# An eighth full set of seven block products, with fewer partner halves spread evenly between them, in a GLA and differential attention layer

## The chip, the cores and the metric

The kernel runs on one core of a Trainium2 chip. The metric is the device time of one launch in microseconds (us). The text names the engines as the profile does: PE is TensorE (PEld its weight loads), DVE is VectorE, ACT is ScalarE, POOL is GpSimd and SP is SyncE. POOL and SP mostly issue DMAs here.

## The reference

One decoder layer on a sequence of 256 tokens and a width of 2048, all in float32. What matters here is how much of it is matrix products:

```
h = rmsnorm(x, pre_norm_g)                       # 256 x 2048
proj = h @ w_in                                  # 2048 columns and more for each of:
(a_q, a_k, a_v, a_g, a_lr, b_q, b_k, b_v, b_g, m_a, m_b) = split(proj)
gk  = log_sigmoid(a_lr @ gla_gk_w2 + gla_gk_b) / 16
o_a = rmsnorm(gla_chunked(a_q, a_k, a_v, gk)) * gla_norm_g * silu(a_g)   # 4 heads
y_a = o_a @ w_branch_a
o_b = rmsnorm(diff_attention(b_q, b_k, b_v, lam)) * diff_norm_g * (1 - 0.2) * silu(b_g)  # 16 heads
y_b = o_b @ w_branch_b
merged = sigmoid(m_a) * y_a + sigmoid(m_b) * y_b
out = x + rmsnorm(merged @ w_out) * post_norm_g
```

The columns a_g, the GLA gates, are called ag0 to ag3 in the kernel (512 columns each). The merge columns m_a are m00 to m03. The queries and keys of the differential heads are dq and dk, in four groups of four heads.

## The kernel before, in words

**Halves.** Weights are read once from DRAM as float32. A float32 product is done as three passes of a reduced-precision one: ScalarE copies a weight tile to the rounded part `hi` (L357), VectorE subtracts it from the tile and keeps the rest `lo` (L358), and TensorE sums hi times the rounded x, hi times the rest of x, and lo times the rounded x. The unit is a *half*, 128 x 1024 weights: one ACT copy, one DVE subtraction, and then the matmuls of L552. All halves stand in one list, `seq` (L208 to L211). `take` (L366) hands out the next half to the matmuls and keeps the splits three halves ahead (`AHEAD`, with three buffers each for hi and lo). `emit_half` (L325) makes the split of one half, and also starts the loads that its place in the list calls for.

**Sets.** Most products h @ w_in are token-major: a half then costs 12 matmuls of 128x512. A *set* computes two groups of 512 columns in a cheaper way: it cuts x and the weights into 2 x 2 blocks and forms seven block products in place of eight (`block_products`, L827, in the order `PRODUCTS` = 1, 3, 5, 6, 2, 7, 4). A half of a set costs 6 matmuls of 128x512 (four with hi, two with lo), and each product of a full set has four halves: two block rows t = 0 and 1, and two halves of each. This text names such a place by product and t, "5.1" for product 5, t = 1. Seven products of 24 matmuls are 168, where two token-major groups take 192. Before, there are seven full sets, 0 to 6, and one *quarter set* that does a quarter of the work of one ag and one merge group (`QUARTER`, ag3 and m02), with two halves for each product.

**The price of a set.** The products need sums of weight blocks. A set has chain tiles in SBUF: a holds block 0 and b block 3, both loaded on POOL's queue by `link` (L224), for the next set's first product during products 7, 4 and 1. After the halves of product 1 are split, `accumulate` (L251, also on POOL's queue) adds block 1 from DRAM onto a, in four pieces of 512 KB for the two tiles (t = 0 and 1), by a DMA that adds into SBUF. Products 1 uses a as loaded, product 5 uses a with block 1 added; products 3 and 7 use b. After product 5's and product 2's halves, and again after 6 and 7, VectorE adds b or the tile c (block 2, loaded by SP's queue into `raws`) onto a (L260), and block 1 is accumulated onto b as well. So product 5's split has to wait for the landing of the accumulates that were issued at product 1.

**Partners.** Between the halves of the sets the list has other halves of w_in, called *partners* here (`others`, L782): the last group of GLA values (v4), the GLA keys and queries, and the differential heads' queries and keys of the groups named in `EARLY`. Their raw tiles come by SP's queue. Except for v4 they are channel-major: their x side is the moving operand, and a half costs 8 matmuls 512 wide and 8 of 256. `phase_steps` (L100) sets the order: after each slot (s, product, t) one partner, but for a list `skip`; in the first four slots one more. Before, there are 105 slots and 88 partners; in sets 1 to 6 a full set of 14 slots has 11 partners (none after 4.0, 2.0 and 1.0; sets 5 and 6 have one less after 4.1), and the quarter set's seven slots have six.

**Evictions and gates.** Products 1, 6, 7 and 4 add into one PSUM bank x. Product 1 and product 5 are copied out to SBUF by ScalarE (`kept`, L871), and VectorE adds those copies to later banks (L874, L878, L882, L886). Sets of merge columns (`MERGE`, sets 0, 1 and 6) end in a Tanh (L837, L845). The others end in a Tanh on ScalarE and one VectorE operation that makes t times (1 + tanh) of it (L840 and L841, and `gate` at L596). The missing factors 1/2 and rstd are put in later, where the heads are normalised. Results are written to DRAM (`spill`, L175 to L179, on POOL's queue) and fetched back when needed. The quarter set's results are fetched as parts and added to the rest of ag3 and m02.

**After the sets** come ag0 to ag3 and m02 as token-major groups, the differential heads of group 3, m03, and then the two branches and the output product. The GLA scores and the attention of the heads are woven into this stretch.

Of the kernel before, what the change touches and what calls it, by code (L numbers as in the profile page):

```python
# [6 lines left out]
F32 = mybir.dt.float32  # L7
# [4 lines left out]
ALU = mybir.AluOpType  # L12
# [17 lines left out]
SETS = 7  # L30
# [3 lines left out]
EARLY = (0, 1, 2)  # L34
# [15 lines left out]
def chunk_plan():  # L50
# [15 lines left out]
    plan.append(("set6", "set", "w_in", [(o + 8192, 1024)]))  # L66
    plan.append((f"set{SETS}", "quarter", "w_in", [(5632, 512), (o + 9216, 512)]))
    for g in range(4):
        plan.append((f"ag{g}", "rest" if g == 3 else "tok", "w_in", [(4096 + 512 * g, 512)]))
# [30 lines left out]
def phase_steps():  # L100
# [7 lines left out]
    skip = [(SETS, 4, 0), (SETS - 1, 4, 1), (SETS - 2, 4, 1)] + [(s, prod, 0) for prod in (4, 2, 1) for s in range(SETS - 1, 0, -1)]  # L108
    skip = skip[: len(slots) + len(front) - len(other)]
    mixed = []  # L110
    for slot in slots:
        mixed += [("set", *slot, h) for h in range(2)]
        for _ in range((slot not in skip) + (slot in front)):
            mixed.append(other.pop(0))
# [29 lines left out]
def hybrid_kernel(ctx: ExitStack, tc, xt, xn, preg, postg, w, w2, gkb, glag, lamv, diffg, ident_d, causal_d, lmask_d, out):  # L144
# [64 lines left out]
    seq += halves_of(*(f"ag{g}" for g in range(4)))  # L209
    seq += halves_of("m02") + heads_order(3) + halves_of("m03", *(f"y0{g}" for g in range(4)))[:-4]  # L210
# [237 lines left out]
    const.tile([P, 24], F32, name="margin")  # L448
# [12 lines left out]
    def norm():  # L461
# [12 lines left out]
        dve.tensor_scalar(out=half_rstd, in0=rstd, scalar1=0.5, scalar2=None, op0=ALU.mult)  # L474
        dve.tensor_scalar(out=minus_half, in0=rstd, scalar1=-0.5, scalar2=None, op0=ALU.mult)
# [120 lines left out]
    def gate(bank, b, dst):  # L596
        t = t2([P, 512], "tanh")
        act.activation(t, bank, AF.Tanh, scale=half_rstd[:, b : b + 1])
        dve.scalar_tensor_tensor(out=dst, in0=t, scalar=1.0, in1=bank, op0=ALU.add, op1=ALU.mult)
# [227 lines left out]
    def block_products(s):  # L827
        x = ps("mm")
        bank = {1: x, 6: x, 7: x, 4: x}
        kept, halves = {}, {}  # L830

        def right_done(b):
# [5 lines left out]
            else:  # L838
                t = t2([P, 512], "tanh")
                act.activation(t, dst, AF.Tanh, scale=half_rstd[:, b : b + 1])  # L840
                dve.scalar_tensor_tensor(out=dst, in0=t, scalar=-1.0, in1=dst, op0=ALU.add, op1=ALU.mult)  # L841

        def left_done(b, src):
            if s in MERGE:
                act.activation(halves["l"][:, b, :], src, AF.Tanh, scale=half_rstd[:, b : b + 1])  # L845
            elif s < SETS:
                act.activation(halves["l"][:, b, :], src, AF.Copy, scale=rstd[:, b : b + 1])
            elif b:
                act.activation(halves["l"][:, b, :], src, AF.Copy)

        for prod in PRODUCTS:
# [4 lines left out]
            for t in range(few):  # L856
                for h in range(2):
                    hi, lo = take(("set", s, prod, t, h))
                    for w, parts in ((hi, (0, 1)), (lo, (0,))):
                        for j in range(2):  # L860
                            kt = 4 * t + 2 * h + j
                            a = operand(prod, kt)
                            for part in parts:
                                first = prod not in (6, 7, 4) and kt == 0 and w is hi and part == 0
# [805 lines left out]
```

## Time and profile before

| | |
|---|---|
| median of 3 runs | 1089.87 us (1087.65 to 1090.18) |
| the profiled execution: its span | 1087.3 us (no other time is given for it) |
| busy, PE / DVE / ACT / POOL | 1079.5 / 930.8 / 720.0 / 154.5 us |
| DMA | 288.21 MB, 265 GB/s in the mean |
| granted TensorE clock | full speed in each of the 40 slices |

The span is the time from the first to the last instruction of one profiled execution. The median of the other runs is 2.6 us above it. A group's row in the profile gives the line, engine, operation, the output and input tiles, how many there were, the busy time and the mean length of one (ns), and behind the second bar the idle time of the engine before them with what ended it. A row of a timeline gives start, length, engine, line, operation and tiles, and in brackets how long the engine was idle before it and what released it. "DMA to landing" gives the time from the issue of a DMA to its last byte.

### The profile page before, as it was taken

Reading aid. Unit: us, or ns where it says so; the run is one execution under the profiler, and the core shown is the slowest. Engines: PE = TensorE matmul, PEld = TensorE weight load, DVE = VectorE, ACT = ScalarE, POOL = GpSimd, SP = SyncE. Lnnn points to the kernel's source line nnn. Section 1 sums busy time; section 2 is a strip of 40 time slices with the busy share of each in tenths; the row PEclk is TensorE's granted clock in tenths of the full one; section 3 lists DMA queues with packets and bytes.
Section 4 is the critical chain, followed back from the end, with each engine's and each line's share of the span. In section 5 each row is a group of like instructions: output and inputs, shape, how many; then the busy total and the mean of one; then the engine's idle time right before and its main releaser. Section 6 shows DMA issues by size and latency. Waiting matters only on the chain.

```text
span 1087.3 us, 15367 instructions
## 1 busy us (share of the span) xinstructions
PE 1079.5 (99%) x5440; PEld 925.4 (85%) x5440; DVE 930.8 (86%) x1295; ACT 720.0 (66%) x1047; POOL 154.5 (14%) x229
## 2 busy tenths in 40 slices
PE   9999999999999999999999999999999999999997
PEld 8999888888888888888888888888888888888886
DVE  7787987979979899798998899877778878889886
ACT  7886766676766767667676465556777767566662
POOL 0201112121121211212102100021011011100000
PEclk9999999999999999999999999999999999999999
DMA  9889869799797997979968656599898898988752
GB/s 351 286 296 331 241 252 295 210 354 224 258 272 213 364 243 269 295 190 365 241 242 248 239 181 208 180 326 324 259 297 258 280 298 261 333 293 264 272 187 104
DMA packets 64941, 288.21 MB, mean 265 GB/s; under 512 B 8480, under 2 KB 11552, under 8 KB 46944
## 3 DMA queue, kind: packets, MB, share of 16 engines
q1 hardware_dynamic: 39520, 183.72, 48.2%
q0 software_dynamic: 24768, 102.77, 34.6%
q8 instruction: 43, 0.70, 0.3%
q10 hardware_dynamic: 576, 0.73, 0.2%
q14 instruction: 34, 0.28, 0.1%
HBM read 260.98 MB, written 26.21 MB: 264 GB/s over the span
## 4 chain that ended last, share of the span: by engine, by line
PE 88%; issue 5%; DMA 4%; DVE 2%; POOL 1%; ACT 0%; POOLq 0%; ACTq 0%; DVEq 0%
PE mm L552 54%; PE bg L552 24%; DMA a<-in_w_dram 2%; PE mm L540 2%; PE bg L540 2%; PE mm L525 1%; PE bg L977 1%; DVE lo L358 1%; DMA b<-in_w_dram 1%; PE bg L525 1%; DMA dl<-dk 1%; PE bg L1145 0%; PE bg L1119 0%; PE bg L444 0%; PE bg L1120 0%
## 5 line engine op out<-in xcount | busy, mean ns | idle before, releaser
L357 ACT ACTIVATE hi<-raw 128x1024 fp32r<-128x1024 f32 (+3 forms) x253 | 259.2, 1031 | 185.8 <-PE bg L552 89.9
L358 DVE TENSOR_TENSOR lo<-raw,hi 128x1024 fp32r<-128x1024 f32 (+3 forms) x255 | 300.3, 1183 | 63.9 <-ACT hi L357 59.3
L552 PE MATMUL mm<-hi,xs 128*128 128x512 f32 (+1 forms) x808 | 204.3, 386 | 0.0
L552 PEld LDWEIGHTS mm<-hi,xs 128*128 128x128 f32 x808 | 149.7, 188 | 25.0 <-ACT hi L357 0.2
L358 DVE TENSOR_TENSOR lo<-a,hi 128x1024 fp32r<-128x1024 f32 x120 | 144.7, 1220 | 23.7 <-ACT hi L357 22.9
L552 PE MATMUL bg<-xs,hi 128*128 128x512 f32 x640 | 164.9, 389 | 0.0
L357 ACT ACTIVATE hi<-a 128x1024 fp32r<-128x1024 f32 x120 | 127.0, 1060 | 47.2 <-PE mm L552 27.4
L552 PEld LDWEIGHTS bg<-xs,hi 128*128 128x128 f32 x640 | 120.3, 188 | 23.4
L552 PE MATMUL mm<-lo,xs 128*128 128x512 f32 (+1 forms) x404 | 113.1, 384 | 0.3 <-DVE lo L358 0.2
L552 PEld LDWEIGHTS bg<-xs,lo 128*128 128x128 f32 x640 | 87.2, 190 | 6.3
L552 PE MATMUL bg<-xs,lo 128*128 128x256 f32 x640 | 89.2, 282 | 0.0
L552 PEld LDWEIGHTS mm<-lo,xs 128*128 128x128 f32 x404 | 75.5, 188 | 14.6 <-DVE lo L358 1.1
L358 DVE TENSOR_TENSOR lo<-b,hi 128x1024 fp32r<-128x1024 f32 x60 | 72.4, 1221 | 6.5 <-ACT hi L357 5.0
L357 ACT ACTIVATE hi<-b 128x1024 fp32r<-128x1024 f32 x60 | 63.5, 1061 | 17.0 <-PE mm L552 14.7
L552 PE MATMUL mm<-hi,oah 128*128 128x512 f32 x128 | 50.8, 397 | 0.0
L552 PE MATMUL mm<-hi,oal 128*128 128x512 f32 x128 | 50.0, 391 | 0.0
L251 POOL DMA_DIRECT2D b<-in_w_dram x30 | 26.0, 869 | 138.5 <-DVE a L260 112.1
L1131 ACT ACTIVATE prob<-prob,mx,score_scale 128x128 f32<-128x128 f32 x64 | 34.3, 539 | 8.2 <-DVE mx L1126 8.0
L552 PE MATMUL mm<-hi,obh 128*128 128x512 f32 x96 | 37.7, 393 | 0.0
L552 PE MATMUL mm<-hi,obl 128*128 128x512 f32 x96 | 37.4, 390 | 0.0
L260 DVE TENSOR_TENSOR a<-a,b 128x1024 f32<-128x1024 f32 x30 | 36.3, 1221 | 0.3
L357 ACT ACTIVATE hi<-c 128x1024 fp32r<-128x1024 f32 x30 | 31.7, 1057 | 7.1 <-PE mm L552 4.9
(417 smaller groups left out, 2066.8 us busy)
## 6 DMA issues: line engine op xcount, KB each, us to landing
raw<-in_w_dram SPq DMA_DIRECT2D x110, 1024.0 KB, 6.8
a<-in_w_dram POOLq DMA_DIRECT2D x30, 512.0 KB, 12.6
c<-in_w_dram SPq DMA_DIRECT2D x30, 512.0 KB, 8.5
b<-in_w_dram POOLq DMA_DIRECT2D x30, 512.0 KB, 8.2
a<-in_w_dram POOLq DMA_DIRECT2D x13, 1024.0 KB, 8.5
b<-in_w_dram POOLq DMA_DIRECT2D x13, 1024.0 KB, 8.6
raw<-in_w_dram SPq DMA_DIRECT2D x14, 832.0 KB, 7.1
gr<-gr POOLq DMA_DIRECT2D x8, 512.0 KB, 7.9
```

The source lines that it names most:

```text
L251: pool.dma_start(chain[s, name, i][:, c], block(s, 1, i)[:, c], accum_op=ALU.add)
L260: dve.tensor_tensor(out=a, in0=a, in1=chain[s, "b", i][:, c] if second else raws[s, i, h], op=ALU.add)
L357: act.activation(hi_t[:, a:b], r[:, a:b], AF.Copy)
L358: dve.tensor_tensor(out=lo_t[:, a:b], in0=r[:, a:b], in1=f32(hi_t[:, a:b]), op=ALU.subtract)
L525: i = pe.matmul(out, lhs, rhs, start=first and n == 0, stop=last and n == len(pairs) - 1, **kw)
L540: i = pe.matmul(banks[g][b][:, :n], a[part][:, P * b : P * b + P], w[:, n * g : n * g + n], start=first, stop=last)
L552: i = pe.matmul(*args, **kw)
L977: pe.matmul(o, xk[:, P * c : P * c + P], xq.rearrange("p (b c t) -> p b c t", b=2, c=4)[:, :, c, :], start=i == 0, stop=i == 1)
L1131: act.activation(prob[m][:, lo:up], prob[m][:, lo:up], AF.Exp, scale=score_scale[:, b : b + 1], bias=mx[:, i : i + 1], accum_out=z[:, i : ...
```

## The change

1. `SETS` becomes 8. Set 7 does ag0 and ag1 (`GLA_GATES`), which leave the token-major part; the quarter set becomes set 8. The results of set 7 are spilled, with the gate already applied, and fetched back where ag0 and ag1 were computed.
2. Partners stand by a fixed table: in a full set after 3.0, 5.1, 6.0, 6.1, 2.1, 7.0, 7.1 and 4.1, which are 8 for a set, and in the quarter set after products 5, 6, 2 and 7, which are 4. `EARLY` is (0, 1), so the heads of group 2 are no longer partners; they follow m02, ahead of those of group 3. There are now 119 slots and 72 partners.
3. Gates are one Silu on ScalarE with rstd as its scale, in place of a Tanh and a VectorE operation. With that the factor 1/2 and rstd are no longer put in at the heads' normalisation, and two small VectorE multiplications go.
4. In sets 1 and later ScalarE's copy of product 1 goes to a second PSUM bank in place of SBUF, and product 2's matmuls add onto it, so VectorE's addition (L882) goes.

The built program has 3628 matmuls of 128x512 where there were 3652; all other matmuls keep their numbers. It has eight loads of ScalarE's function table where there were two (at L385 and L837). In the new ones Silu alternates with the exponential of the attention (L959 of the changed file); between the Tanh of set 6 and the Silu of set 7 none stands. Line numbers shift by four to nine: the subtraction is L362, the copy L361, the accumulate L255.

```diff
-SETS = 7
+SETS = 8
+GLA_GATES = 7
 QUARTER = ("ag3", "m02")
 MERGE = (0, 1, 6)
-EARLY = (0, 1, 2)
+EARLY = (0, 1)
+PARTNERED = ((3, 0), (5, 1), (6, 0), (6, 1), (2, 1), (7, 0), (7, 1), (4, 1))
+LAST_PARTNERED = (5, 6, 2, 7)
...
     plan.append(("set6", "set", "w_in", [(o + 8192, 1024)]))
+    plan.append((f"set{GLA_GATES}", "set", "w_in", [(4096, 1024)]))
     plan.append((f"set{SETS}", "quarter", "w_in", [(5632, 512), (o + 9216, 512)]))
...
-    skip = [(SETS, 4, 0), (SETS - 1, 4, 1), (SETS - 2, 4, 1)] + [(s, prod, 0) for prod in (4, 2, 1) for s in range(SETS - 1, 0, -1)]
-    skip = skip[: len(slots) + len(front) - len(other)]
     for slot in slots:
         mixed += [("set", *slot, h) for h in range(2)]
-        for _ in range((slot not in skip) + (slot in front)):
+        s, prod, t = slot
+        with_partner = prod in LAST_PARTNERED if s == SETS else (prod, t) in PARTNERED
+        for _ in range(with_partner + (slot in front)):
             mixed.append(other.pop(0))
...
-    seq += halves_of(*(f"ag{g}" for g in range(4)))
-    seq += halves_of("m02") + heads_order(3) + halves_of("m03", *(f"y0{g}" for g in range(4)))[:-4]
+    seq += halves_of("ag2", "ag3", "m02") + heads_order(2) + heads_order(3) + halves_of("m03", *(f"y0{g}" for g in range(4)))[:-4]
...
     def gate(bank, b, dst):
-        t = t2([P, 512], "tanh")
-        act.activation(t, bank, AF.Tanh, scale=half_rstd[:, b : b + 1])
-        dve.scalar_tensor_tensor(out=dst, in0=t, scalar=1.0, in1=bank, op0=ALU.add, op1=ALU.mult)
+        act.activation(dst, bank, AF.Silu, scale=rstd[:, b : b + 1])
...
     def block_products(s):
+        seeded = s > 0
...
-                t = t2([P, 512], "tanh")
-                act.activation(t, dst, AF.Tanh, scale=half_rstd[:, b : b + 1])
-                dve.scalar_tensor_tensor(out=dst, in0=t, scalar=-1.0, in1=dst, op0=ALU.add, op1=ALU.mult)
+                act.activation(dst, dst, AF.Silu, scale=minus_rstd[:, b : b + 1])
...
+            elif s == GLA_GATES:
+                gate(src, b, halves["l"][:, b, :])
             elif s < SETS:
...
-                                first = prod not in (6, 7, 4) and kt == 0 and w is hi and part == 0
+                                first = prod not in ((6, 7, 2, 4) if seeded else (6, 7, 4)) and kt == 0 and w is hi and part == 0
...
-                        if prod in (1, 5):
+                        if prod == 1 and seeded:
+                            bank[2] = ps("mm")
+                            act.activation(bank[2], x, AF.Copy)
+                        elif prod in (1, 5):
...
-                            dve.tensor_tensor(out=halves["l"][:, 0, :], in0=out, in1=kept[1], op=ALU.add)
-                            left_done(0, halves["l"][:, 0, :])
+                            if not seeded:
+                                dve.tensor_tensor(out=halves["l"][:, 0, :], in0=out, in1=kept[1], op=ALU.add)
+                            left_done(0, out if seeded else halves["l"][:, 0, :])
...
-            dve.tensor_tensor(out=ssq, in0=ssq, in1=half_rstd, op=ALU.mult)
...
-            dve.tensor_tensor(out=e, in0=e, in1=half_rstd, op=ALU.mult)
...
-    for g in range(4):
+    for g in range(2):
+        gates.append(fetch(gspill[2 * GLA_GATES + g], "ua", u2))
+    for g in (2, 3):
...
-    diff_heads(3)
+    for g in (2, 3):
+        diff_heads(g)
```

VectorE's order in set 5, from the last split of product 1 (the first row, tile a) to the first split of product 5 (the last row, tile a again). In between, b is a split of product 3, raw that of a partner, and the rows with dk or dq belong to the heads. Before:

```order
L358 TENSOR_TENSOR lo_4085<-a_3958,hi_4084 128x1024
L774 TENSOR_TENSOR dk_3986<-dk_3986,rstd_bc 128x256
L358 TENSOR_TENSOR lo_4096<-raw_4082,hi_4095 128x1024
L358 TENSOR_TENSOR lo_4106<-b_3988,hi_4105 128x1024
L358 TENSOR_TENSOR lo_4116<-b_3988,hi_4115 128x1024
L358 TENSOR_TENSOR lo_4129<-raw_4082,hi_4128 128x1024
L358 TENSOR_TENSOR lo_4150<-b_4030,hi_4149 128x1024
L358 TENSOR_TENSOR lo_4162<-b_4030,hi_4161 128x1024
L358 TENSOR_TENSOR lo_4172<-raw_4159,hi_4171 128x1024
L772 TENSOR_TENSOR dk_3986<-bg_4127,dk_3986 128x256
L358 TENSOR_TENSOR lo_4202<-a_3905,hi_4201 128x1024
```

The same stretch of set 5 on VectorE after the change:

```order
L362 TENSOR_TENSOR lo_3622<-a_3494,hi_3621 128x1024
L362 TENSOR_TENSOR lo_3633<-b_3521,hi_3632 128x1024
L783 TENSOR_TENSOR dq_3426<-dq_3426,dh_3613 128x512
L362 TENSOR_TENSOR lo_3645<-b_3521,hi_3644 128x1024
L362 TENSOR_TENSOR lo_3655<-raw_3642,hi_3654 128x1024
L362 TENSOR_TENSOR lo_3668<-b_3563,hi_3667 128x1024
L362 TENSOR_TENSOR lo_3678<-b_3563,hi_3677 128x1024
L362 TENSOR_TENSOR lo_3690<-a_3448,hi_3689 128x1024
```

Between the last split of product 1 and the first of product 5 there were three partners and there is one; a fourth one stood, and stands no more, between 5.0 and 5.1 (behind the last row).

POOL's order in set 6, from the accumulates onto a (L251) to those onto b; gl, dh and dl are spills of results to DRAM. Before:

```order
L251 DMA a_4520<-in_w_dram 128x1024 x2
L251 DMA a_4563<-in_w_dram 128x1024
L178 DMA gl_4669<-gl_4494 128x1024
L251 DMA a_4563<-in_w_dram 128x1024
L251 DMA b_4591<-in_w_dram 128x1024 x2
L251 DMA b_4633<-in_w_dram 128x1024 x2
```

The same on POOL after the change:

```order
L255 DMA a_3979<-in_w_dram 128x1024 x2
L183 DMA gl_4119<-gl_3955 128x1024
L255 DMA a_4025<-in_w_dram 128x1024
L183 DMA dh_4147<-dh_4144 128x512
L183 DMA dl_4149<-dq_3957 128x512
L255 DMA a_4025<-in_w_dram 128x1024
L255 DMA b_4052<-in_w_dram 128x1024 x2
L255 DMA b_4094<-in_w_dram 128x1024 x2
```

The spill of the last set's left half has moved ahead of the third accumulate, and the two spills of a head pair now stand between the third and the fourth.

## The prediction on record

> **What bounds the kernel now.** I read the page's busy times and slices first, then the list of what PE waited for, then windows of the sets, and last the timelines of PE, ACT and POOL around the accumulates. The page of before:
>
> ```profile
> span 1087.3 us, 15367 instructions
> PE 1079.5 (99%) x5440; PEld 925.4 (85%) x5440; DVE 930.8 (86%) x1295; ACT 720.0 (66%) x1047; POOL 154.5 (14%) x229
> PEclk9999999999999999999999999999999999999999
> ```
>
> PE is busy 99% of the span at the full granted clock in all 40 slices. What PE waited for, in us, times, and the longest:
>
> ```profile
> PE bg L444 <- DVE ones_b L441: 1.6, 1, 1.6
> PE bg L1608 <- ACT diag L1607: 1.0, 1, 1.0
> PE mm L552 <- DVE lo L358: 0.4, 2, 0.2
> ```
>
> The first is the start, the second the end; between them PE loses 0.4 us. So the time is the sum of the matmuls, and a change moves it in two ways only: by the number of matmuls, and by new waits of PE. All other engines matter only as far as they make PE wait. How far they are from that, in one 60 us window inside the sets and two short ones in set 5 (columns: length, busy time of PE, PEld, DVE, ACT, POOL, granted clock, DMA share, GB/s):
>
> ```profile
> 480.00:540.00 60.00, 60.00 (x300) 50.98 (x299) 54.47 (x56) 42.42 (x48) 13.67 (x20) 1.00 0.87 273
> 438.00:446.00 8.00, 8.00 (x41) 6.77 (x40) 5.93 (x7) 5.81 (x8) 4.02 (x5) 1.00 1.00 388
> 446.00:462.00 16.00, 16.00 (x84) 13.67 (x82) 12.37 (x14) 10.18 (x13) 1.14 (x2) 1.00 0.93 249
> ```
>
> DVE is 91% busy, ACT 71%, and the DMA engines 87%. Where only plain loads run they move 388 GB/s at a share of 1.00; where the accumulates run (446 to 462) a share of 0.93 moves only 249. The sets live close to what the DMA engines can move.
>
> **What a half and a partner cost.** PE's timeline in set 5, from product 1 to product 3 with one partner (bg) between:
>
> ```profile
> 440.00 1.09 PE L552 MATMUL mm<-hi,xs 128*128 128x512 f32 x4
> 440.93 0.62 PE L552 MATMUL mm<-lo,xs 128*128 128x512 f32 x2
> ...
> 442.74 1.07 PE L552 MATMUL mm<-hi,xs 128*128 128x512 f32 x4
> ...
> 444.10 1.07 PE L552 MATMUL mm<-hi,xs 128*128 128x512 f32 x4
> ...
> 445.46 1.98 PE L552 MATMUL bg<-xs,hi 128*128 128x512 f32 x8
> ...
> 448.23 0.40 PE L552 MATMUL mm<-hi,s4h 128*128 128x512 f32 x1
> ```
>
> A set's half takes 444.10 - 442.74 = 1.36 us for six matmuls, 0.227 us each. A partner takes 448.23 - 445.46 = 2.77 us. The lo matmuls begin 0.93 us after the hi ones.
>
> **Term 1, the matmuls.** The eighth set takes 24 matmuls of 128x512 away: 24 x 0.227 = -5.4 us. All others stay, only in another order.
>
> **Term 2, the accumulates of the full sets.** Partners do two things: they use PE time, and they give the accumulates onto tile a time to land. From the last half of 1.1 to that of 5.1 there were four partners (after 1.1, 3.0, 3.1, 5.0); now there is one (after 3.0). So three go, 3 x 2.77 = 8.3 us. In the rows below POOL issues the last accumulate of sets 1, 2, 4 and 6 and of both halves of the quarter set:
>
> ```profile
> 169.06 0.84 POOL L251 DMA_DIRECT2D a<-in_w_dram  x1 [0.62 <-DVE lo L358]
> 237.31 0.86 POOL L251 DMA_DIRECT2D a<-in_w_dram  x1 [1.01 <-DVE lo L358]
> 374.93 0.85 POOL L251 DMA_DIRECT2D a<-in_w_dram  x1 [1.02 <-DVE lo L358]
> 511.29 1.71 POOL L251 DMA_DIRECT2D a<-in_w_dram  x1
> 572.07 0.90 POOL L251 DMA_DIRECT2D a<-in_w_dram  x1 [5.30 <-DVE lo L358]
> 573.20 0.88 POOL L251 DMA_DIRECT2D a<-in_w_dram  x1 [0.24 <-DVE lo L358]
> ```
>
> PE uses that piece in the last half of product 5 of the same set:
>
> ```profile
> 190.93 0.39 PE L552 MATMUL mm<-hi,r1h 128*128 128x512 f32 x1
> 259.73 0.39 PE L552 MATMUL mm<-hi,r1h 128*128 128x512 f32 x1
> 397.35 0.39 PE L552 MATMUL mm<-hi,r1h 128*128 128x512 f32 x1
> 532.17 0.39 PE L552 MATMUL mm<-hi,r1h 128*128 128x512 f32 x1
> 583.05 0.40 PE L552 MATMUL mm<-hi,r1h 128*128 128x512 f32 x1
> 584.43 0.39 PE L552 MATMUL mm<-hi,r1h 128*128 128x512 f32 x1
> ```
>
> And how long the accumulates of those sets took from issue to landing (set 1, 2, 4, 6, and the quarter set with its two):
>
> ```profile
> DMA to landing us min/median/max: 9.9/13.9/18.6
> DMA to landing us min/median/max: 7.7/11.2/13.8
> DMA to landing us min/median/max: 9.7/13.9/15.6
> DMA to landing us min/median/max: 8.5/12.6/17.3
> DMA to landing us min/median/max: 8.0/8.7/9.4
> ```
>
> The first landing in each row is the least and the last the most, since they queue behind one another. That ACT already waits for them shows that there is little to give:
>
> ```profile
> ACT hi L357 <- DMA a<-in_w_dram: 6.7, 4, 2.3
> ...
> 528.72 1.06 ACT L357 ACTIVATE hi<-a 128x1024 fp32r<-128x1024 f32 x1 [1.26 <-DMA a<-in_w_dram]
> ```
>
> How late may a piece land? ACT's copy takes 1.06 us, DVE's subtraction 1.22 (rows below), and the hand-over between them some 0.1 by my estimate; lo is needed 0.93 after hi. So it has to land 1.06 + 1.22 + 0.1 - 0.93 = 1.45 us before PE's use. With the 8.3 us gone:
>
> - set 1: 190.93 - 169.06 - 8.3 - 1.45 = 12.1 allowed, 18.6 needed: 6.5 late
> - set 2: 259.73 - 237.31 - 8.3 - 1.45 = 12.65, 13.8: 1.15 late
> - set 4: 397.35 - 374.93 - 8.3 - 1.45 = 12.65, 15.6: 2.95 late
> - set 6: 532.17 - 511.29 - 8.3 - 1.45 = 11.1, 17.3: 6.2 late
>
> The mean is 4.2 us, and seven such sets would give 29.4 us. That is the upper bound: it leaves the landing as long as it was. But a queue with three partners fewer carries less. Of the three, I take one raw tile of 1024 KB (two halves) out of the time before the landing; at 388 GB/s it took 2.7 us. Then 3.8, 0, 0.25 and 3.5 us are left, mean 1.9, times seven 13.2 us. The lower bound is 0: if the whole 8.3 us came back from the queue, nothing is late. I take 13.2, as sets 1 and 6 would need most of 6 us of relief, and as in sets 5 to 7 the head spills now stand ahead of the last accumulate on POOL. A wait of ACT here holds up all splits behind it, so PE stops as soon as the three split halves ahead are used; that cover is in the sum already.
>
> **Term 3, the quarter set.** No partner stands between its products 1 and 5 now; two stood there. The first piece: 583.05 - 572.07 - 5.5 - 1.45 = 4.0 us allowed, 8.0 needed, 4.0 late. The second: 584.43 - 573.20 - 5.5 - 1.45 = 4.3, 9.4 needed, 5.1 late, with the first's wait in it. I take 2.5 of the 5.1: a partner stands just ahead, the queue is lighter. The bounds are 0 and 5.1.
>
> **Terms at nothing.** DVE's splits come this closely:
>
> ```profile
> 444.23 1.22 DVE L358 TENSOR_TENSOR lo<-raw,hi 128x1024 fp32r<-128x1024 f32 x1
> 445.37 1.22 DVE L358 TENSOR_TENSOR lo<-b,hi 128x1024 fp32r<-128x1024 f32 x1
> ```
>
> One each 1.14 us. A full set had 28 + 11 splits and 8 additions, 47 x 1.14 = 53.6 us in 28 x 1.36 + 11 x 2.77 = 68.6 us of PE; now it has 44, 50.2 us in 60.2 us. That is 78% before and 83% after without the smaller operations, and those get fewer. The Silu takes the Tanh's place on ACT, and these leave DVE, off PE's path, so they are worth nothing by themselves:
>
> ```profile
> L841 DVE SCALAR_TENSOR_TENSOR gr<-tanh,gr 128x512 f32<-128x512 f32 x8 | 5.5, 685 | 0.0
> L871 ACT ACTIVATE p<-mm 128x512 f32<-128x512 f32 x16 | 9.2, 577 | 0.0
> ```
>
> The copy of product 1 into PSUM has a row only for SBUF, 577 ns. Its price lies between nothing, since 12 halves of a set (16 us) stand between product 1 and product 2, and 0.6 us for each of eight sets if PE had to wait; I take nothing. The fetches of set 7's gates and the moved heads of group 2 keep their PE work; DVE has more to do there beside the GLA scores, so 0 to 2 us, and I take 0.
>
> The six further table loads are bounded by the one in the sets:
>
> ```profile
> L837 ACT ACT_TABLE_LOAD x1 | 1.3, 1283 | 0.0
> ```
>
> 6 x 1.283 = 7.7 us of an engine 66% busy, spread over places with three split halves ahead of PE: I take 0, and up to 2 us in the range. The Trainium skill speaks against this edit: "ScalarE: Activation LUTs", section "What ACT_TABLE_LOAD costs", puts a switch at 1283 ns and a drain of about 1380 ns, which by that page's figures would be an estimated 16 us of ACT. The load's length agrees with this row; the drain does not show in this trace as a row of its own.
>
> **The sum.** -5.4 + 13.2 + 2.5 = +10.3 us. On the profiled span, 1087.3 + 10.3 = 1097.6 us; the median of the runs stands 2.6 us above that span, so the forecast is 1100.2, said as 1100.
>
> **Rivals.**
>
> *Faster: the accumulates land in time.* The landing is long because the queue is full, and half a set's partners' loads are what fills it; if they land 6.5 us sooner, nothing is late. For: the DMA share was 0.87, not 1. Against: within a set PE time falls from 68.6 to 60.2 us while 10 MB of block loads stay, so the demand for each us rises. Then -5.4 stands alone: 1084.5, up to 1086.5 with the small terms. Chance 0.22.
>
> *No change: only the quarter set and about 0.4 us a set.* 2.5 + 7 x 0.4 = 5.3 cancels the 5.4: 1089.8. Chance 0.13.
>
> *Slower by DVE.* Between 5.1 and 7.0 DVE has additions and splits at nearly each half. If it falls short by one 1.14 us operation a set, and the accumulates are in time, that is 7 x 1.14 = 8.0: 1087.3 - 5.4 + 8.0 + 2.6 = 1092.5, with the 2.5 of term 3 1095.0. It decides from one operation more than fits between two halves on. Chance 0.05.
>
> *Slower still by the clock.* A start after idle is slow:
>
> ```profile
> 1.60 4.45 PE L444 MATMUL bg<-ones_b 128*128 128x512 bf16 x10 [1.60 <-DVE ones_b L441]
> ```
>
> Ten matmuls took 4.45 us, 445 ns each, against 227 later: 2.2 us lost for one restart. If PE's stalls in three sets were long enough to bring that back, 3 x 2.2 = 6.6 goes on top: 1106.8. The slices show no drop so far, as no stall is longer than 0.2 us. Chance 0.04. The Trainium skill, "TensorE: Matmul & The Clock Gate", section "HAM oscillation — how this bites in real kernels", sets the point at PE gaps of more than about 3.4 us; no run here shows it yet.
>
> **How the numbers follow.** The forecast's own chance is 0.56, with its own range from 1093 (above the 0.3%, about 3.3 us, that a measurement of this kernel can tell from no change) to 1112 (two thirds of the way to the bound without relief: 1087.3 - 5.4 + 29.4 + 5.1 + 2.6 = 1119). The range reaches down to the faster rival: 1084 to 1112. Faster is that rival, 0.22; same 0.13; slower 0.56 + 0.05 + 0.04 = 0.65.
>
> **What would show it.** Right: PE's list of waits has new entries of some 10 to 20 us together for lo and hi in the sets, behind ACT waiting for the DMA into a, just at product 5, longest in sets 1, 6 and 7 and in the quarter set; PE's busy time falls by about 5.4. Wrong: landings of 8 to 12 us for the last accumulate, ACT's wait for a near 6.7 us as before, PE still 99% busy. If PE waits for lo with DVE behind additions between 5.1 and 7.0, the DVE rival holds; a granted clock below 1.00 in the sets means the last one.

## The result and the profile after

The changed kernel takes 1115.17 us (median of 4 runs, 1113.57 to 1117.58) against 1088.89 us for the kernel before beside it: a ratio of 1.0239, 95% interval 1.0225 to 1.0252. It is slower by 26 us. The forecast, 1100, had the sign and lies below the result by 15 us; its range ended at 1112. The page after:

```profile
span 1113.8 us, 15403 instructions
PE 1089.5 (98%) x5416; PEld 918.1 (82%) x5416; DVE 939.8 (84%) x1276; ACT 739.5 (66%) x1068; POOL 164.5 (15%) x245
PEclk9999999999999999999999999999999999999999
```

No engine's share tells of the loss. PE's busy time has even grown by 10 us with 24 matmuls fewer, since around a stall the matmuls are recorded longer and further apart (0.50 us and 0.34 apart in the rows at 232.27 and 232.61 below, where 0.39 and 0.23 are usual), so a part of the waiting counts as busy: in the seven sets 1 to 7 PE is busy for 436.90 us, and for 424.32 in the run with plain pieces below. What PE waited for, and the row of ACT's waits (90 to 640 us) that grew most, of the changed kernel:

```profile
PE mm L558 <- ACT hi L361: 12.9, 13, 1.8
PE bg L448 <- DVE ones_b L445: 1.6, 1, 1.6
PE bg L558 <- DVE lo L362: 1.6, 6, 0.3
PE bg L1618 <- ACT diag L1617: 1.0, 1, 1.0
PE mm L558 <- DVE lo L362: 1.0, 3, 0.4
```

```profile
ACT hi L361 <- DMA a<-in_w_dram: 30.9, 16, 2.7
```

PE's 12.9 us of waits for ACT's copies did not exist before, and ACT's waits for the DMA into a went from 6.7 to 30.9 us. Where this stands in the program: the first matmuls of set 1 and of the quarter set,

```profile
149.47 0.86 PE L558 MATMUL mm<-hi,xs 128*128 128x512 f32 x3
...
601.14 0.62 PE L558 MATMUL mm<-hi,xs 128*128 128x512 f32 x2
```

so the seven sets between took 451.67 us, 64.5 us each, where halves and partners add up to 60.2. The landings of the accumulates in sets 1, 2, 4, 6 and the quarter set of the changed kernel:

```profile
DMA to landing us min/median/max: 12.1/13.7/15.0
DMA to landing us min/median/max: 12.4/13.8/15.1
DMA to landing us min/median/max: 12.9/14.3/15.3
DMA to landing us min/median/max: 9.4/11.2/12.0
DMA to landing us min/median/max: 5.9/6.5/7.1
```

In set 6 the last piece is issued late, as the prediction read from POOL's order: the one before it at 475.38, the last at 479.15, with the two spills of the heads between:

```profile
475.38 0.85 POOL L255 DMA_DIRECT2D a<-in_w_dram  x1 [1.77 <-DVE lo L362]
...
479.15 0.95 POOL L255 DMA_DIRECT2D a<-in_w_dram  x1
```

Set 2 shows the whole course of a loss. ACT's copies of product 5, each behind a landing:

```profile
224.98 1.06 ACT L361 ACTIVATE hi<-a 128x1024 fp32r<-128x1024 f32 x1 [1.09 <-DMA a<-in_w_dram]
227.44 1.06 ACT L361 ACTIVATE hi<-a 128x1024 fp32r<-128x1024 f32 x1 [1.40 <-DMA a<-in_w_dram]
231.16 1.06 ACT L361 ACTIVATE hi<-a 128x1024 fp32r<-128x1024 f32 x1 [2.66 <-DMA a<-in_w_dram]
233.69 1.06 ACT L361 ACTIVATE hi<-a 128x1024 fp32r<-128x1024 f32 x1 [1.47 <-DMA a<-in_w_dram]
```

All four pieces come late, 2.5 us and 3.7 us apart, so the lead of three halves is used up at the third, where PE stands for 1.39 us, and at the fourth for another 0.54. PE and then VectorE behind it:

```profile
232.27 0.50 PE L558 MATMUL mm<-hi,r1h 128*128 128x512 f32 x1 [1.39 <-ACT hi L361]
232.61 0.39 PE L558 MATMUL mm<-hi,r1l 128*128 128x512 f32 x1
...
234.80 0.50 PE L558 MATMUL mm<-hi,r1h 128*128 128x512 f32 x1 [0.54 <-ACT hi L361]
...
236.63 1.78 PE L558 MATMUL bg<-xs,hi 128*128 128x512 f32 x7
...
242.37 1.98 PE L558 MATMUL bg<-xs,hi 128*128 128x512 f32 x8
244.60 1.22 PE L558 MATMUL bg<-xs,lo 128*128 128x256 f32 x8 [0.26 <-DVE lo L362]
245.66 0.40 PE L558 MATMUL mm<-hi,s2h 128*128 128x512 f32 x1
```

```profile
234.78 1.22 DVE L362 TENSOR_TENSOR lo<-a,hi 128x1024 fp32r<-128x1024 f32 x1 [1.30 <-ACT hi L361]
235.92 1.22 DVE L264 TENSOR_TENSOR a<-a,b 128x1024 f32<-128x1024 f32 x1
237.06 1.22 DVE L362 TENSOR_TENSOR lo<-raw,hi 128x1024 fp32r<-128x1024 f32 x1
...
241.60 1.22 DVE L264 TENSOR_TENSOR a<-a,b 128x1024 f32<-128x1024 f32 x1
242.73 0.68 DVE L882 TENSOR_TENSOR p<-mm,p 128x512 f32<-128x512 f32 x1
```

The last half of product 5 takes 236.63 - 234.80 = 1.83 us instead of 1.36, as its lo, begun at 234.78, ends at 236.00. From there VectorE runs without a gap, one operation on 128x1024 each 1.14 us, and cannot win the lead back: the partner at 242.37 takes 245.66 - 242.37 = 3.29 instead of 2.77, as its lo is late. So a set loses twice: at the landing, and then while VectorE is behind.

### The profile page after: what moved, and what is told of

Read it like the earlier page. It is cut to its first block, busy times and chain, and to the rows that moved or that the text cites. A ratio compares the mean times of both kernels' runs of the same rounds, so it can differ in the third digit from the quotient of the medians.

```text
span 1113.8 us, 15403 instructions
## 1 busy us (share of the span) xinstructions
PE 1089.5 (98%) x5416; PEld 918.1 (82%) x5416; DVE 939.8 (84%) x1276; ACT 739.5 (66%) x1068; POOL 164.5 (15%) x245
## 2 busy tenths in 40 slices
DMA packets 66669, 292.40 MB, mean 263 GB/s; under 512 B 8672, under 2 KB 11744, under 8 KB 49184
## 4 chain that ended last, share of the span: by engine, by line
PE 79%; DMA 10%; DVE 6%; issue 3%; ACT 2%; POOL 1%; POOLq 0%; ACTq 0%; SPq 0%; DVEq 0%
PE mm L558 50%; PE bg L558 19%; DMA a<-in_w_dram 9%; DVE lo L362 3%; PE mm L546 2%; PE bg L546 2%; ACT hi L361 1%; DMA raw<-in_w_dram 1%; DVE a L264 1%; PE mm L531 1%; PE bg L986 1%; PE bg L531 1%; PE bg L1153 0%; PE bg L1127 0%; DVE p L882 0%
## 5 line engine op out<-in xcount | busy, mean ns | idle before, releaser
L361 ACT ACTIVATE hi<-raw 128x1024 fp32r<-128x1024 f32 (+3 forms) x237 | 242.7, 1028 | 148.3 <-PE mm L558 65.9
L362 DVE TENSOR_TENSOR lo<-raw,hi 128x1024 fp32r<-128x1024 f32 (+3 forms) x239 | 281.4, 1183 | 42.8 <-ACT hi L361 39.1
L362 DVE TENSOR_TENSOR lo<-a,hi 128x1024 fp32r<-128x1024 f32 x136 | 165.8, 1221 | 55.1 <-ACT hi L361 51.2
L361 ACT ACTIVATE hi<-a 128x1024 fp32r<-128x1024 f32 x136 | 143.9, 1058 | 83.1 <-DMA a<-in_w_dram 30.9
L558 PE MATMUL mm<-hi,xs 128*128 128x512 f32 (+1 forms) x728 | 184.8, 384 | 0.0
L558 PE MATMUL bg<-xs,hi 128*128 128x512 f32 x512 | 132.5, 391 | 0.0
L558 PEld LDWEIGHTS bg<-xs,hi 128*128 128x128 f32 x512 | 96.7, 189 | 19.3
L362 DVE TENSOR_TENSOR lo<-b,hi 128x1024 fp32r<-128x1024 f32 x68 | 81.3, 1219 | 10.4 <-ACT hi L361 10.4
L361 ACT ACTIVATE hi<-b 128x1024 fp32r<-128x1024 f32 x68 | 71.2, 1058 | 28.5 <-PE mm L558 18.4
L558 PEld LDWEIGHTS bg<-xs,lo 128*128 128x128 f32 x512 | 68.7, 190 | 10.9 <-DVE lo L362 7.1
L558 PE MATMUL mm<-xs,hi 128*128 128x512 f32 x256 | 68.0, 397 | 0.0
L255 POOL DMA_DIRECT2D b<-in_w_dram x34 | 29.2, 859 | 167.4 <-DVE a L264 124.5
L558 PEld LDWEIGHTS mm<-xs,hi 128*128 128x128 f32 x256 | 46.2, 189 | 7.8
L361 ACT ACTIVATE hi<-c 128x1024 fp32r<-128x1024 f32 x34 | 36.0, 1060 | 13.9 <-PE mm L558 10.6
L362 DVE TENSOR_TENSOR lo<-c,hi 128x1024 fp32r<-128x1024 f32 x34 | 41.1, 1216 | 0.0
## 6 DMA issues: line engine op xcount, KB each, us to landing
a<-in_w_dram POOLq DMA_DIRECT2D x34, 512.0 KB, 12.4
```

The source lines that it names most:

```text
L255: pool.dma_start(chain[s, name, i][:, c], block(s, 1, i)[:, c], accum_op=ALU.add)
L361: act.activation(hi_t[:, a:b], r[:, a:b], AF.Copy)
L362: dve.tensor_tensor(out=lo_t[:, a:b], in0=r[:, a:b], in1=f32(hi_t[:, a:b]), op=ALU.subtract)
L558: i = pe.matmul(*args, **kw)
```

## The experiments

Theory W: the accumulates onto a land too late, since three partners went from between 1.1 and 5.1. Rivals: D, VectorE between 5.1 and 7.0; T, the function tables and the copy into PSUM; E, the eighth set itself; and, for what makes the landing late, the queue, the bytes, or the adding.

**Seven sets with the sparse partners** (the new gates, and the partners of the changed kernel):

```diff
 SETS = 7
-EARLY = (0, 1, 2)
+EARLY = (0, 1)
+PARTNERED = ((3, 0), (5, 1), (6, 0), (6, 1), (2, 1), (7, 0), (7, 1), (4, 1))
+LAST_PARTNERED = (5, 6, 2, 7)
...
-        for _ in range((slot not in skip) + (slot in front)):
+        s, prod, t = slot
+        with_partner = prod in LAST_PARTNERED if s == SETS else (prod, t) in PARTNERED
+        for _ in range(with_partner + (slot in front)):
```

> Seven full sets as before, so no matmul is saved, with the new gates, and the partners of the changed kernel: the heads of group 2 go behind m02, and a set has 8 partners at the table's places (8 partner halves that are left over follow the quarter set). Theory W: the places of the partners alone make the loss, some 4 us for each of sets 1 to 6 and 1 to 2 for the quarter set: 1112 to 1119. Rival E (the eighth set itself brings it, by its 14 MB more of blocks, spills and fetches): 1089 to 1095.

1117.72 us, ratio 1.0268 (1.0249 to 1.0287). W holds and E falls: the fewer partners at their new places lose it all without an eighth set, which adds only 4.2 MB to what the DMAs move (292.40 MB after the change, 288.21 before).

**The gates alone**, on the kernel before (edits 3 and 4 of the change, none of 1 and 2):

```diff
-        act.activation(t, bank, AF.Tanh, scale=half_rstd[:, b : b + 1])
-        dve.scalar_tensor_tensor(out=dst, in0=t, scalar=1.0, in1=bank, op0=ALU.add, op1=ALU.mult)
+        act.activation(dst, bank, AF.Silu, scale=rstd[:, b : b + 1])
...
+                            bank[2] = ps("mm")
+                            act.activation(bank[2], x, AF.Copy)
```

> The kernel before, with the Silu gates and with product 1's copy in PSUM, but its own seven sets and its own 88 partners. Theory W: these edits take work off VectorE that no one waits for, and put six table loads on ScalarE that are hidden: 1087 to 1090, no change. Rival T (table loads): 2 to 6 us slower. Rival D: VectorE was already close to the limit before, so 2 to 5 us faster.

1089.12 us beside 1089.02, ratio 1.0004 (0.9994 to 1.0014): no change, though this kernel has 12 table loads where the one before has two. T falls.

**The old gates** in the new arrangement (edits 1 and 2 without 3 and 4):

```diff
-        act.activation(dst, bank, AF.Silu, scale=rstd[:, b : b + 1])
+        act.activation(t, bank, AF.Tanh, scale=half_rstd[:, b : b + 1])
+        dve.scalar_tensor_tensor(out=dst, in0=t, scalar=1.0, in1=bank, op0=ALU.add, op1=ALU.mult)
```

> The eight sets and the new places of the partners, but with the gates, the copy of product 1 and the left sum as before (Tanh on ScalarE and one VectorE operation; copy to SBUF and addition on VectorE). Theory W: the arrangement alone makes the loss, 1112 to 1118. Rival T (function tables, Silu and the copy into PSUM cost ScalarE time that PE waits for): 1100 to 1108. Rival D: VectorE's extra additions in the tight stretch make it slower still, 1120 to 1130.

1123.43 us, ratio 1.0306 (1.0282 to 1.0329), 8 us more than the changed kernel. W alone expected no difference; D has a part. By the starts of the halves in the seven sets, products 2 and 7, where VectorE's additions stand, lose 4.5 us more than in the changed kernel. Not all of the 8 us is VectorE's: in 10 us windows of the profiled execution the granted clock fell in three places, which cost some 5 us together, where the changed kernel lost 1.7 in one. The same edits that are worth nothing where VectorE is hidden are worth some 4.5 us where it has to catch up.

**No accumulates onto a:**

```diff
         if prod == 1:
-            accumulate("a", t)
```

> The changed kernel without the accumulates onto a (block 1 is left out of those sums, so products 5, 6 and 4 use fewer blocks; all matmuls and splits stay). Theory W: all of the loss goes with the wait, time 1084 to 1089, which is what 24 matmuls fewer give. Rival D: the part of the loss that lies between 5.1 and 7.0 (in the changed kernel's trace about 0.8 to 1 us a set at products 6, 2 and 7) stays: 1090 to 1094.

1087.22 us, ratio 0.9982 (0.9971 to 0.9993): 28 us less than the changed kernel. PE's waits at product 5 go, and with them what followed at products 6, 2 and 7. So VectorE's part is the aftermath of the landing, not a bound of its own. The sets also move fewer bytes here; the next run keeps them.

**Plain in place of adding**: block 1 overwrites a, by the same bytes on the same queue at the same place.

```diff
-            pool.dma_start(chain[s, name, i][:, c], block(s, 1, i)[:, c], accum_op=ALU.add)
+            pool.dma_start(chain[s, name, i][:, c], block(s, 1, i)[:, c], **({"accum_op": ALU.add} if name == "b" else {}))
```

> The changed kernel, with block 1 written over a by a plain DMA of the same size on the same queue at the same place, in place of an adding one (products 5, 6 and 4 then lack block 0 in their sums; matmuls and splits stay; the additions onto b stay). Theory A (adding in the DMA is what takes 2.5 us for each 512 KB): four plain pieces land in some 9 us in place of 12 to 15, and the waits at product 5 go: 1087 to 1093. Theory B (bytes from DRAM set it, adding costs nothing): 1110 to 1116.

1089.38 us, ratio 1.0000 (0.9990 to 1.0009). In the full sets it is the adding that makes the landing too late. The four pieces of set 2 now take

```profile
DMA to landing us min/median/max: 10.0/10.6/11.1
```

so the last one lands 4 us sooner, and PE has no wait at product 5. The quarter set is an exception: it takes 32.6 us with plain pieces and 32.4 with adding ones, and ACT still waits 2.3 us for a piece, so there the window is too short for either. Windows of set 2 in which the pieces were under way, of the changed kernel and of this one (columns as in the prediction):

```profile
221.00:229.00 8.00, 8.00 (x41) 6.72 (x40) 6.97 (x7) 4.70 (x6) 0.00 (x0) 1.00 1.06 250
229.00:234.00 5.00, 3.54 (x15) 2.19 (x13) 1.99 (x2) 1.37 (x2) 0.86 (x1) 1.00 1.07 211
```

```profile
216.00:224.00 8.00, 8.00 (x40) 6.74 (x40) 7.40 (x7) 5.90 (x8) 0.00 (x0) 1.00 0.93 377
```

These figures count all queues, but in the trace at least 95% of the bytes in these windows are POOL's. With the adding pieces the engines are full at 211 to 250 GB/s; with plain ones they move 377 at a share of 0.93.

**Four partners in the window**:

```diff
-PARTNERED = ((3, 0), (5, 1), (6, 0), (6, 1), (2, 1), (7, 0), (7, 1), (4, 1))
+PARTNERED = ((1, 1), (3, 0), (3, 1), (5, 0), (5, 1), (6, 0), (2, 1), (7, 0))
```

> The changed kernel with the eight partners of a full set at other places: after 1.1, 3.0, 3.1, 5.0, 5.1, 6.0, 2.1 and 7.0. Theory W (the window): what costs the time is that three partners went from between 1.1 and 5.1, so that the accumulates onto a land too late for product 5. With them back the window is 8.3 us longer, landings of 12 to 15 us fit, and the 20 to 25 us go: 1089 to 1096 us. Rival D (VectorE): the stretch from 5.1 to 7.0, with its additions, is what costs; it has two partners less than in the changed kernel (none after 6.1 and 7.1), so the time stays at 1112 or rises. Rival Q (POOL's queue): the next set's loads of a and b, with no partner after 7.1 and 4.1, come late in turn, and PE waits at products 1 and 3: 1100 to 1110.

1115.24 us, ratio 1.0229 (1.0207 to 1.0252): no gain, but not for D's reason. The waits at product 5 did go; in their place PE has a wait that neither theory named:

```profile
PE mm L558 <- DVE gr L895: 14.6, 8, 1.8
```

L895 reads bank x after product 7, and product 4 adds onto that bank next. Without a partner after 7.1 PE waits for the reading, 1.8 us in each of eight sets. Behind three of these waits the granted clock fell too (0.83 in 210 to 220 and in 270 to 280 us, 0.94 and 0.89 in 520 to 540): by the starts of the halves product 4 lost 3.7 us in those sets, and 2.05 in the others.

**Three in the window, and one after 7.1**:

```diff
+PARTNERED = ((1, 1), (3, 0), (3, 1), (5, 1), (6, 0), (2, 1), (7, 0), (7, 1))
```

> The changed kernel with partners after 1.1, 3.0, 3.1, 5.1, 6.0, 2.1, 7.0 and 7.1: against the first rearrangement, which had no wait left at product 5 but 2.1 us a set before product 4, the one after 5.0 goes to 7.1, where it gives VectorE time to read bank x before product 4 adds onto it again. Theory W (window before product 5, and cover for the reading of x after product 7): both waits are gone, as two partners more than in the changed kernel give 5.5 us, and the stage falls to some 61 us a full set: 1088 to 1093 us. Rival D: with none after 6.1, VectorE is late at products 2 and 7: 1095 to 1105. Rival Q (whatever is gained at one place is lost at the next, as the DMA engines can't bring 14 MB a set in 60 us): 1105 to 1115.

1103.95 us, ratio 1.0138 (1.0118 to 1.0157): 11 us won. W's 1088 to 1093 was not reached. By the starts of the sets, 2 to 4 take 60.4 to 61.1 us, as W has it, although their last pieces land after 15.8 to 16.5 us; sets 5 to 7 take 63.5 to 64.9.

**And the quarter set's partners after 3, 5, 2, 7**:

```diff
-LAST_PARTNERED = (5, 6, 2, 7)
+LAST_PARTNERED = (3, 5, 2, 7)
```

> As the one before, and the quarter set's four partners after products 3, 5, 2 and 7 in place of 5, 6, 2 and 7. Theory W: the quarter set's wait at product 5 (1.4 us in the changed kernel) goes, 1 to 2 us less than the run beside it. Rival: no difference, since the wait moves to product 6 with VectorE's additions.

1103.50 us, ratio 1.0130 (1.0110 to 1.0151), the same as beside it. The wait at product 5 shrinks, another at product 2 comes up.

**The heads' spills on SP's queue**, with three partners in the window and one after 7.1:

```diff
-        return spill(hi, "dh"), spill(t, "dl")
+        return spill(hi, "dh", sp), spill(t, "dl", sp)
```

> The run with partners after 1.1, 3.0, 3.1, 5.1, 6.0, 2.1, 7.0 and 7.1 took 61 us for each of sets 1 to 4, but 64 to 65 for sets 5 to 7, where the spills of the heads stand between the accumulates on POOL. Here those spills go on SP's queue. Theory W with the spills: sets 5 to 7 fall to some 61 us, 1091 to 1096. Rival (SP's queue is held up by the spill's wait for VectorE, and the raw loads come late): 1103 to 1115.

1099.35 us, ratio 1.0098 (1.0080 to 1.0116), the fastest of the eight-set kernels that compute all. Sets 5 to 7 fall to 62.3 to 63.6 us each, 1.3 us in the mean where 3.4 were expected; the spills between the accumulates are a part of what sets 5 to 7 lose.

**One more partner in the window**, from after 6.1 to after 3.1:

```diff
+PARTNERED = ((3, 0), (3, 1), (5, 1), (6, 0), (2, 1), (7, 0), (7, 1), (4, 1))
```

> The changed kernel with one partner of each full set moved from after 6.1 to after 3.1, so into the window before product 5. Theory W: the window is 2.8 us longer, where the waits at product 5 are 1.7 to 2.9 us a set and the delays behind them at products 6 to 7 another 0.8 to 1: 12 to 20 us less, 1095 to 1103. Theory D (VectorE between 5.1 and 7.0 needs the partner at 6.1): 1108 to 1116, with the waits moved to products 2 and 7.

1116.51 us, ratio 1.0250 (1.0234 to 1.0266). W's expectation failed outright. The landings in set 2 are now

```profile
DMA to landing us min/median/max: 12.9/14.8/18.1
```

with 18.1 us for the last, against 15.1: the partner brings 2.77 us of PE time, but a raw load as well. SP issues the next one at 225.53, while the pieces are under way, where the changed kernel issues it at 238.30, and the last piece comes 3 us later. So this window is hardly wider; with two partners more in it, in the runs above, it was. The granted clock fell in three places in this run, some 5 us in all against 1.7, so without that the time is still some 2 us from the changed kernel's and not 12 to 20.

**Half of the partners' loads left out**:

```diff
+        if key in spare and r == 0 and spare.index(key) % 2:
+            raws[key, r] = raws[spare[spare.index(key) - 1], r]
+            return
```

> The changed kernel with every second raw load of the partners left out (16 of 32 loads of 1024 KB; such a partner uses the weights of the one before it, all splits and matmuls stay), which is about 2 MB less for each full set. Theory B (the DMA engines' bandwidth sets when the accumulates land, so a load less in the window lets them land some 2.7 us sooner, as the prediction took it): 1092 to 1102. Theory S (the accumulates run at a pace of their own on their queue, whatever SP loads): 1110 to 1116.

1104.61 us, ratio 1.0143 (1.0122 to 1.0163), between the two theories. In set 2, with about one load of 1024 KB less ahead of it, the last piece lands after 12.1 us instead of 15.1. Over sets 1 to 4 it is 12.1 to 13.0 instead of 15.0 to 15.3, so a load in the window is worth 2 to 3 us, about what the prediction took; in sets 5 to 7, where the issue is late and the landing was 12 us already, it hardly moves.

```profile
DMA to landing us min/median/max: 9.4/10.8/12.1
```

**The loads of b on SP's queue**:

```diff
-        (pool if s else sp).dma_start(c, block(s, {"a": 0, "b": 3}[name], t))
+        (pool if s and name == "a" else sp).dma_start(c, block(s, {"a": 0, "b": 3}[name], t))
```

> The changed kernel with the loads of b (1 MB each, two a set) on SP's queue, so that the accumulates onto a do not stand behind them on POOL's. Theory W with the queue as the limit: the accumulates land some 5 us sooner, and 15 to 20 us go: 1095 to 1100. Theory W with the DMA engines' bandwidth as the limit: the same bytes go through the same engines, the landing moves by under 2 us, time 1110 to 1116. Rival D: no change, 1113 to 1117.

1111.97 us, ratio 1.0205 (1.0187 to 1.0224), 3 us less; in the profiled execution these lie in sets 5 to 7. In set 2 the first piece lands after 8.8 us instead of 12.4, the last after 15.2 as before:

```profile
DMA to landing us min/median/max: 8.8/13.1/15.2
```

The place in the queue matters little for the last piece, as the theory of shared bandwidth had it.

**The loads of c behind the accumulates**, in program order on POOL's queue, in three kernels: the changed one; the one with the heads' spills on SP; and the changed one with spills on SP and the quarter set's partners after 3, 5, 2, 7.

```diff
-            sp.dma_start(raws[s, i, j], block(s, 2, i)[:, 1024 * j : 1024 * j + 1024])
+            tc.keep_in_program_order(pool.dma_start(raws[s, i, j], block(s, 2, i)[:, 1024 * j : 1024 * j + 1024]))
...
-            pool.dma_start(chain[s, name, i][:, c], block(s, 1, i)[:, c], accum_op=ALU.add)
+            tc.keep_in_program_order(pool.dma_start(chain[s, name, i][:, c], block(s, 1, i)[:, c], accum_op=ALU.add))
```

> The changed kernel with the loads of c (block 2, 2 MB a set) on POOL's queue, in program order behind the accumulates onto a. In the changed kernel SP issues them some 10 to 15 us before the accumulates, and they land just as those start. Theory C (the backlog of plain loads ahead of the accumulates, and c's above all, sets when they begin): the accumulates land up to 2 MB at 388 GB/s = 5.4 us sooner, the waits at product 5 (2 to 3 us a set) and what follows them go, 1086 to 1093. Theory S (the four adding pieces' own 10 us and the loads of b set it): 1105 to 1116.

> The same with the partners after 1.1, 3.0, 3.1, 5.1, 6.0, 2.1, 7.0 and 7.1 and the heads' spills on SP's queue. Theory C: all of sets 1 to 7 run at some 60.5 us, and only the quarter set's 3 us are left: 1084 to 1089, at or below the kernel before. Theory S: no better than with c on SP, 1096 to 1101.

> The changed kernel with c on POOL's queue as in the first of these runs, its own places for the partners of the full sets, the heads' spills on SP's queue and the quarter set's partners after products 3, 5, 2 and 7. Theory C: the three known waits are all met, 1083 to 1088. Theory S: 1100 to 1112.

The first, 1105.77 us, ratio 1.0151 (1.0136 to 1.0167), takes 9 us less than the changed kernel, a third of the loss, and misses its expectation by 13. The last piece of set 2 lands after 11.5 us:

```profile
DMA to landing us min/median/max: 9.0/10.4/11.5
```

Set 2 is the best of them; in sets 1, 3 and 4 it is 12.8 to 13.8 us, against 15.0 to 15.3. So c's early loads were a part of the backlog, but not all of it. The second, 1109.06 us, ratio 1.0181 (1.0157 to 1.0206), missed by 20 us. In its full sets the waits at product 5 are gone, and ACT waits for c at product 2 in their place:

```profile
ACT hi L361 <- DMA c<-in_w_dram: 23.4, 10, 3.0
ACT hi L361 <- DMA a<-in_w_dram: 13.5, 8, 2.8
```

In its profiled execution (1111.90 us) the granted clock fell in three stretches, which cost some 7 us; an execution with a mean clock of 0.999 took 1105.86. The third, 1105.02 us, ratio 1.0141 (1.0124 to 1.0158), is the same as the first, and missed by 17. No arrangement of the eight sets that I tried beats the kernel before, and what would is open: where one wait was cured, another showed, at the reading of a bank, at c, or at product 2 of the quarter set.

## Why the prediction was partly right

The change cost 26.3 us where 10.3 were forecast, beyond the end of the range. The path was the forecast one; its size was not.

**The bound and the sign: right.** PE's time is matmuls and waits; the new waits are for the accumulates at product 5, with ACT behind the DMA into a. Taking the accumulates away takes 28 us away, plain ones in their place 26.

**Term 2, 13.2 us: the step that failed.** Between the starts of set 1 and the quarter set the changed kernel takes 451.67 us. Without the accumulates it is 574.34 - 149.63 = 424.71:

```profile
149.63 0.62 PE L556 MATMUL mm<-hi,xs 128*128 128x512 f32 x2
...
574.34 0.62 PE L556 MATMUL mm<-hi,xs 128*128 128x512 f32 x2
```

So the term is 27.0 us. That it comes close to the bound without relief, 29.4, is in part luck: that bound took landings that were 4.2 us late in the mean, where 2.8 were measured (below), and had nothing for VectorE or the clock. What failed first is the relief, "I take one raw tile of 1024 KB (two halves) out of the time before the landing". A load less is worth about that much, but the landings did not follow: the last piece took 15.0 us instead of 18.6 in set 1, but 15.1 instead of 13.8 in set 2, where the first piece took 12.4 instead of 7.7. What shares the engines with the pieces is more than the partners' loads: with c's 2 MB a set behind them they landed 1.2 to 3.6 us sooner. With the measured landings the same sums give 15.0 - 12.1 = 2.9 us late in set 1, 15.1 - 12.65 = 2.45 in set 2 and 15.3 - 12.65 = 2.65 in set 4. In set 6 it is 12.0 - 11.1 = 0.9, and the spills that I named but did not price held up the issue besides: 479.15 - 475.38 = 3.77 us behind the piece before it, where halves follow one another in 1.36, so 2.4 us more, 3.3 in all. The mean is 2.8 where 1.9 was taken, and seven times that is 19.8 us. What failed second is that this was taken for the whole loss. By the starts of the halves, against the sets without accumulates, 22.0 us of the 27.0 lie at product 5 with the partner behind it, 1.6 of them by the clock in set 7 (below). The other 5.1 lie at products 6, 2 and 7, where VectorE is catching up as in the rows of set 2; the sum had no term for that.

**Term 1, -5.4: right as a count, not reached.** The sets without accumulates run at 424.71 / 7 = 60.7 us, against 60.2. But that kernel is at 1087.22 beside 1089.01, so only 1.8 us of the 5.4 are seen. By the starts of the halves, 0.8 us go in each of sets 1 and 4 at product 3, where ACT waits for b; where the other 2 go is open. With the accumulates left out the change was worth 0.2%, and with plain ones in their place nothing. The measured terms add up: 27.0 + 1.7 - 1.8 = 26.9 against 26.3.

**Term 3, 2.5: right in kind.** The quarter set took 32.4 us, and 30.7 without accumulates: 1.7. With plain pieces it took 32.6, so here the adding is not what cost; with a partner after product 3 the wait at product 5 shrank, as shown above.

**Terms at nothing: right alone, wrong together.** The Silu, the copy into PSUM and the table loads change nothing on the kernel before. The Trainium skill ("ScalarE: Activation LUTs", "What ACT_TABLE_LOAD costs") gives some 1283 ns for a table load, and each load took that here too. Ten more of them made no difference on the kernel before, where ScalarE is 66% busy. The drain that the prediction named beside it finds no room in the changed kernel's trace: an activation ends at 658.78 us, a load runs from 658.79 to 660.07, and the next activation starts at 660.09. But in the new arrangement the work taken from VectorE is worth some 4.5 us, which my ledger by whole sets (78% and 83%) could not show. It had to be made for the stretch behind the stall, where VectorE runs without a gap.

**The rivals.** Faster and no change fell with W's waits. VectorE as a bound of its own fell with the two kernels without adding transfers onto a, where it is in time; as aftermath it is about a fifth of the 27.0 us. The clock's rival came once in the changed kernel:

```profile
550.00:560.00 10.00, 8.16 (x29) 5.91 (x28) 6.05 (x6) 4.82 (x5) 1.27 (x2) 0.84 0.62 135
```

In set 7 the granted clock was 0.84 for 10 us, 1.6 us lost behind a wait of 1.8: real, and small. Behind the other waits of 1 to 2 us in the sets of this run it stayed at 1.00. In three of the kernels tried (four partners in the window, one more partner, the old gates) it fell in three places, some 5 us for each kernel.

## What to carry to other kernels

Work that stands between a DMA's issue and its use is a cover: before it is moved, take the landing from the trace and sum what is left, without credit for a lighter queue unless a run has shown it. A stall costs more than its length if an engine behind it has little to spare in that stretch, so make its ledger for the stretch and not for the loop. And ask of fill brought in to cover a transfer what it loads itself: one more partner bought nothing here, two more did.

## What the runs showed of the hardware

While DMAs that add into SBUF were under way the engines were full at 211 to 250 GB/s, where the same bytes written plainly moved at 377; in this kernel that was worth 26 us. The granted clock fell behind a single wait of 1.8 us, though the Trainium skill ("TensorE: Matmul & The Clock Gate", "HAM oscillation — how this bites in real kernels") speaks of gaps of more than about 3.4 us. These are the matmuls of 128x512 behind that wait in the changed kernel, 0.42 us apart instead of 0.23:

```profile
556.73 0.80 PE L558 MATMUL mm<-hi,r1h 128*128 128x512 f32 x1 [1.77 <-ACT hi L361]
557.33 0.63 PE L558 MATMUL mm<-hi,r1l 128*128 128x512 f32 x1
557.75 0.63 PE L558 MATMUL mm<-hi,r1h 128*128 128x512 f32 x1
558.18 0.63 PE L558 MATMUL mm<-hi,r1l 128*128 128x512 f32 x1
```

With four partners in the window the clock fell behind three of eight waits of 1.8 us, and each time some 1.65 us more were lost.
